# Modulation as row sums on the vector engine, and gate and up products with stationary weights, in a two-block kernel

## The chip, the core and the metric

The kernel runs on one core of a Trainium2 chip, in float32 throughout, in one launch. Five engines run their own instruction streams in order and meet through semaphores: PE (matrix products; PEld is its loading of stationary operands), DVE (vector), ACT (activation functions), POOL, and SP, whose queue here only starts transfers. The metric is the device time of an execution in microseconds (us). The median of three executions of the kernel before is 2738.47 us (2736.33 to 2739.03).

## The reference

256 tokens of width 2048 pass through two blocks; the parts that the change touches:

```python
c_act = jax.nn.silu(c)                                   # c: [1, 2048]
mod = (c_act @ ada_w + ada_b)                            # ada_w: [2048, 6 * 2048]
sh1, sc1, g1, sh2, sc2, g2 = jnp.split(mod, 6, axis=-1)

h = rms_norm(x, norm1_g) * (1 + sc1) + sh1
proj = h @ w_in + b_in                                   # w_in: [2048, 11264]
...                                                      # LRU and attention branches, merged
x = x + g1 * (merged @ w_o)
h2 = rms_norm(x, norm2_g) * (1 + sc2) + sh2
gate, up = jnp.split(h2 @ w_ffn_in, 2, axis=-1)          # w_ffn_in: [2048, 2 * 5632]
x = x + g2 * ((jax.nn.silu(gate) * up) @ w_ffn_out)
x = rms_norm(x, final_g)
...                                                      # second block: gated linear attention
h2 = rms_norm(x, norm_g_2[1])
gate, up = jnp.split(h2 @ ffn_w_gu_2, 2, axis=-1)
x = x + (jax.nn.silu(gate) * up) @ ffn_w_down_2
```

## The kernel before

Activations lie transposed in SBUF: features on the 128 partitions, the 256 tokens along the row, four feature tiles to a buffer `[128, 4, 256]`. `act` holds 24 such slots.

**Products.** Every large weight is read once, in chunks of 512 x 512 (1 MB) that SP starts into `raw` (three buffers). A chunk is split into two float32r parts: ACT copies half a chunk, `[128, 1024]`, to `hi` (L173), and DVE subtracts, `lo = raw - hi` (L175). There are three buffers for each of `hi` and `lo`, so these run up to three halves ahead of PE. A chunk then takes three products, hi x hi, hi x lo and lo x hi, for each of its four 128-row tiles (`accumulate`). In one form the weights are stationary: 128 x 128 of them are loaded, and 256 tokens stream past (L197, L199, L201), 48 matmuls of 256 columns a chunk; the result has features on the partitions. In the other (`tokens=True`) the activations are stationary and 512 weight columns stream past (L190 to L192), 24 matmuls of 512 columns; the result has tokens on the partitions. There are 464 chunks, so 928 splits on DVE. `split` asks the scheduler for high priority (`PREP`), so splits are placed ahead of other work on ACT and DVE.

**Stages.** First the input products of `h` for 10 column groups of `w_in` (40 chunks, accumulators `e` and `part`; the plan goes through the four 512-feature pieces `h[0]` to `h[3]` in turn, so that the first products need `h[0]` alone), with attention after them; then `w_attn_out` (`aops`), the other groups of `w_in` with the LRU (`ups`, `gps`, `glps`), `w_lru_out` (`lops`), `w_o` (`wops`), the first feed-forward layer (`fgps` gate, `fups` up, `fops` down), the second block, and its feed-forward layer.

**Modulation.** `ada_w` has 12 strips of 1024 columns. `matvec` (L234) goes through a strip in 16 steps: each loads 128 rows, `[128, 1024]` (512 KB), into `mvw` (five buffers) and adds them, times the partition's `silu(c)` value, to `mva` on DVE (L245 the first, L247 the others). After the last step PE sums `mva` over the partitions against a column of ones (`reduce`, L259: eight float32 matmuls of one column, which the trace shows as 16 records), and DVE adds the bias into `mod` (L274). Strip 0 runs before anything else. Strips 1 to 3, which each complete the next `h`, run between the input products, their loads started by POOL; strips 4 to 11 are doled out by `pump()` (a credit per chunk) into the stages up to the first feed-forward layer, their loads on SP's queue, among the chunks of `raw`. One more `matvec` makes `fb`, what `shift2` adds to the first gate group, as a row (L255).

**Feed-forward layers.** `swiglu` takes 11 groups of 512 hidden features, six and then five. Gate and up products run in the `tokens` form; ACT takes SiLU of the gate (L718, L963), DVE multiplies by the up product (L724, L969). Since the down product needs features on the partitions, `turned` sends the result back through PE, eight 128 x 128 transposes a group (L666), and ACT and DVE make the hi and lo parts from PSUM (L668, L669). `by_token` (L336) transposes the two norms' factors.

What decides order: instructions are recorded in program order and a scheduler places them on each engine by its own estimate and the priorities; each engine then works through its list in order.

Of the kernel before, what the change touches and what calls it, by code (L numbers as in the profile page):

```python
# [11 lines left out]
F32 = mybir.dt.float32  # L12
# [13 lines left out]
SLOTS, MVS, RAWS, HIS, LOS = 24, 5, 3, 3, 3  # L26
# [9 lines left out]
    ("c", 16), ("norm1_g", 16), ("b_in", 88), ("conv_w", 64), ("conv_b", 16),  # L36
# [13 lines left out]
def block_pair_kernel(ctx: ExitStack, tc: tile.TileContext, a: dict):  # L50
# [47 lines left out]
    x = [xpool.tile([P, 4, T], F32, name=f"x{g}") for g in range(NG)]  # L98
    ident = const.tile([P, P], F32, name="ident")
# [130 lines left out]
    cact = const.tile([P, 16], F32, name="cact")  # L230
    nc.scalar.activation(cact, v("c", 0, 16), AF.Silu)
    mod = const.tile([P, 96], F32, name="mod")

    def matvec(srcs, col, width, done, queue=nc.gpsimd, row=False):  # L234


        state = {}

        def step(k):
            def run():  # L240
                w = mvw.tile([P, width], F32, tag="mvw", name="mvw")
                queue.dma_start(w, srcs[k])
                if k == 0:
                    state["acc"] = slot("mva", shape=[P, width])
# [6 lines left out]
        def reduce():  # L251
            n = width // P
            ps = bank("mvp")
            if row:
                nc.tensor.matmul(ps[:, 0:width], ones, state["acc"], start=True, stop=True)  # L255
                done(ps[:, 0:width])
                return
            for f in range(n):
                nc.tensor.matmul(ps[:, f:f + 1], state["acc"][:, f * P:(f + 1) * P],  # L259
                                 ones[:, 0:1], start=True, stop=True)  # L260
            done(ps[:, 0:n])

        return [step(k) for k in range(NK)] + [reduce]

    def ada_steps(strip, queue=nc.gpsimd):


        def done(ps):
            if strip < 4:
                cols = ((16 + 4 * strip, 0, 4), (4 * strip, 4, 4))  # L270
            else:
                cols = ((8 * strip, 0, 8),)
            for j, p, n in cols:
                nc.vector.tensor_tensor(mod[:, j:j + n], ps[:, p:p + n], v("ada_b", j, n), ALU.add)  # L274

        return matvec([a["ada_w"][strip, k] for k in range(NK)], lambda k: cact[:, k:k + 1],
                      1024, done, queue)
# [34 lines left out]

    def normed(g, gain, inv, shift, name):
        t = slot(name + "t")
        p = Pair(name)
        for f in range(4):
            j = 4 * g + f
            sh = shift[:, j:j + 1]
            nc.vector.scalar_tensor_tensor(t[:, f, :], x[g][:, f, :], gain[:, j:j + 1], inv,
                                           ALU.mult, ALU.mult)  # L320
            nc.scalar.activation(p.hi(f), t[:, f, :], AF.Identity, bias=sh)
            nc.vector.scalar_tensor_tensor(p.lo(f), t[:, f, :], sh, f32(p.hi(f)),
                                           ALU.add, ALU.subtract)
        return p
# [102 lines left out]
    first = ada_steps(0, nc.sync)  # L427
    for st in first[:10]:
        st()
    for g in range(NG):  # L430
        nc.sync.dma_start(x[g], a["xT"][g])
    for st in first[10:]:
        st()
# [5 lines left out]
    h = []  # L439

    def next_h():
        q = len(h)
        sl = slice(4 * q, 4 * q + 4)
        nc.vector.scalar_tensor_tensor(gain1[:, sl], mod[:, 16 + 4 * q:20 + 4 * q], 1.0,
                                       v("norm1_g", 4 * q, 4), ALU.add, ALU.mult)
        h.append(normed(q, gain1, inv1, shift1, "h"))

    next_h()
    nc.sync.dma_start(ident, a["ident"])
    nc.sync.dma_start(amask, a["amask"])  # L450
    bv = slot("bv", shape=[P, 512])
    nc.sync.dma_start(bv, a["bv"])
# [8 lines left out]
    early = {}  # L461
    ga = {}
    attn = []
# [610 lines left out]
```

## Time and profile before

| | |
|---|---|
| median of three executions | 2738.47 us |
| the profiled execution | 2733.5 us, of which its span 2731.7 us |
| instructions in the span | 43911 |
| read from memory | 597.06 MB, 219 GB/s over the span |
| first product of the input stage | 44.86 us |
| last matmul to the end of the span | 4.0 us |

A row of the profile's timeline gives the start and the duration in us, the engine, the line, the operation and its tiles as out<-in. Matmuls overlap, so what one costs is the distance between starts, not its duration. A row of the windows gives a stretch, its length, the busy time of each engine with its count of instructions, the granted clock of PE (1.00 is full), and what the 16 DMA engines did.

### The profile page before, as it was taken

The numbers are of one execution on the slowest core, as the hardware profiler recorded it, in microseconds if no ns is written. First come the engines' busy times: TensorE is split into PE (matmuls) and PEld (weight loads), VectorE is DVE, ScalarE is ACT, GpSimd is POOL, SyncE is SP. The second block draws the span as 40 slices with busy tenths as digits, with TensorE's granted clock in tenths as the row PEclk, the third lists the DMA queues.
The fourth block names the chain that finished last, engine by engine and source line by source line (L and its number), as shares of the span: only waits on it lengthen the run. The fifth ranks groups of instructions, "written<-read, shape, count | busy, mean of one in ns | idle before, by whom it ended". The sixth has DMA issues, their size and how long they took to land.

```text
span 2731.7 us, 43911 instructions
## 1 busy us (share of the span) xinstructions
PE 2680.5 (98%) x18612; PEld 2479.3 (91%) x18612; DVE 1782.3 (65%) x2000; ACT 1310.7 (48%) x1525; POOL 25.7 (1%) x52
## 2 busy tenths in 40 slices
PE   4999999999999999999999999999999999999999
PEld 3999999999999888999888999899988889988899
DVE  8887876888887865444545667866654544444544
ACT  3446637864445444434444545655544444344443
POOL 1100000000000000000000000000000000000000
PEclk9999999999999999999999999999999999999999
DMA  9984696769875866555555544444555555555554
GB/s 351 370 311 147 221 341 226 273 243 351 336 278 194 311 238 217 186 200 187 191 192 185 195 170 170 142 152 171 200 186 187 195 188 188 199 186 194 190 195 161
DMA packets 100166, 602.00 MB, mean 220 GB/s; under 512 B 11121, under 2 KB 11633, under 8 KB 40577
## 3 DMA queue, kind: packets, MB, share of 16 engines
q1 hardware_dynamic: 93056, 574.03, 59.1%
q0 software_dynamic: 6912, 25.17, 2.3%
q8 instruction: 145, 2.38, 0.3%
q14 instruction: 53, 0.43, 0.0%
HBM read 597.06 MB, written 2.10 MB: 219 GB/s over the span
## 4 chain that ended last, share of the span: by engine, by line
PE 95%; DVE 2%; issue 1%; DMA 1%; ACT 1%; SPq 0%; DVEq 0%; ACTq 0%
PE fgps L192 6%; PE fgps L191 6%; PE fgps L190 6%; PE fops L197 6%; PE fups L190 6%; PE fups L192 6%; PE fups L191 6%; PE fops L201 6%; PE fops L199 6%; PE part L197 2%; PE part L199 2%; PE part L201 2%; PE lops L201 1%; PE ups L197 1%; PE wops L197 1%; PE ups L201 1%
## 5 line engine op out<-in xcount | busy, mean ns | idle before, releaser
L175 DVE TENSOR_TENSOR lo<-raw,hi 128x1024 fp32r<-128x1024 f32 x928 | 1134.3, 1224 | 842.9 <-ACT hi L173 841.2
L173 ACT ACTIVATE hi<-raw 128x1024 fp32r<-128x1024 f32 x928 | 983.1, 1060 | 1270.4 <-PE fups L192 274.5
L197 PE MATMUL fops<-hid,hi 128*128 128x256 f32 x1408 | 389.0, 276 | 0.0
L201 PE MATMUL fops<-hid,lo 128*128 128x256 f32 x1408 | 388.7, 276 | 0.0
L199 PE MATMUL fops<-hid,hi 128*128 128x256 f32 x1408 | 388.6, 276 | 0.0
L190 PE MATMUL fups<-hi,h 128*128 128x512 f32 x704 | 274.0, 389 | 0.0
L192 PE MATMUL fups<-hi,h 128*128 128x512 f32 x704 | 273.9, 389 | 0.0
L191 PE MATMUL fups<-lo,h 128*128 128x512 f32 x704 | 273.9, 389 | 0.0
L199 PEld LDWEIGHTS fops<-hid,hi 128*128 128x128 f32 x1408 | 264.3, 188 | 0.1
L197 PEld LDWEIGHTS fops<-hid,hi 128*128 128x128 f32 x1408 | 264.3, 188 | 0.2
L201 PEld LDWEIGHTS fops<-hid,lo 128*128 128x128 f32 x1408 | 264.3, 188 | 0.0
L190 PE MATMUL fgps<-hi,h 128*128 128x512 f32 x672 | 263.5, 392 | 0.0
L192 PE MATMUL fgps<-hi,h 128*128 128x512 f32 x672 | 261.8, 390 | 0.0
L191 PE MATMUL fgps<-lo,h 128*128 128x512 f32 x672 | 261.6, 389 | 0.0
L247 DVE SCALAR_TENSOR_TENSOR mva<-mvw,cact,mva 128x1024 f32<-128x1024 f32 x180 | 230.6, 1281 | 26.6 <-DMA mvw<-ada_w 24.5
L191 PEld LDWEIGHTS fups<-lo,h 128*128 128x128 f32 x704 | 132.2, 188 | 27.4
L190 PEld LDWEIGHTS fups<-hi,h 128*128 128x128 f32 x704 | 132.2, 188 | 27.4
L192 PEld LDWEIGHTS fups<-hi,h 128*128 128x128 f32 x704 | 132.2, 188 | 27.4
L192 PEld LDWEIGHTS fgps<-hi,h 128*128 128x128 f32 x672 | 126.1, 188 | 26.2
L190 PEld LDWEIGHTS fgps<-hi,h 128*128 128x128 f32 x672 | 126.2, 188 | 25.6
L191 PEld LDWEIGHTS fgps<-lo,h 128*128 128x128 f32 x672 | 126.2, 188 | 25.5
L197 PE MATMUL part<-h,hi 128*128 128x256 f32 x512 | 145.2, 284 | 0.0
(322 smaller groups left out, 5410.7 us busy)
## 6 DMA issues: line engine op xcount, KB each, us to landing
raw<-w_in SPq DMA_DIRECT2D x88, 1024.0 KB, 5.7
raw<-w_ffn_in SPq DMA_DIRECT2D x88, 1024.0 KB, 4.9
raw<-ffn_w_gu SPq DMA_DIRECT2D x88, 1024.0 KB, 4.8
mvw<-ada_w SPq DMA_DIRECT2D x144, 512.0 KB, 7.0
raw<-gla_w_in SPq DMA_DIRECT2D x48, 1024.0 KB, 4.9
raw<-w_ffn_out SPq DMA_DIRECT2D x44, 1024.0 KB, 4.8
raw<-ffn_w_down SPq DMA_DIRECT2D x44, 1024.0 KB, 4.9
mvw<-ada_w POOLq DMA_DIRECT2D x48, 512.0 KB, 8.5
```

The costliest lines, as they stand in the source:

```text
L173: nc.scalar.activation(hi, rb, AF.Copy)
L175: nc.vector.tensor_tensor(lo, rb, f32(hi), ALU.subtract)
L190: nc.tensor.matmul(ps[t], xh, hi[:, wk, :], start=fst, stop=False)
L191: nc.tensor.matmul(ps[t], xh, lo[:, wk, :], start=False, stop=False)
L192: nc.tensor.matmul(ps[t], xl, hi[:, wk, :], start=False, stop=lst)
L197: nc.tensor.matmul(o, hi[:, wk, wsl], src.hi(kk), start=fst and f % 2 == 0, stop=False, skip_group_check=True)
L199: nc.tensor.matmul(o, hi[:, wk, wsl], src.lo(kk), start=False, stop=False, skip_group_check=True)
L201: nc.tensor.matmul(o, lo[:, wk, wsl], src.hi(kk), start=False, stop=lst, skip_group_check=True)
L247: nc.vector.scalar_tensor_tensor(state["acc"], w, col(k), state["acc"], ALU.mult, ALU.add)
```

## The change

Two edits, and what follows from them.

**Modulation.** `ada_w` is laid out transposed on the host, so that each of 96 tiles has 128 outputs on the partitions and the 2048 inputs along the row, in two halves of 1024 (512 KB each, so as many loads as before). `silu(c)` is laid out as a row, the same on every partition: `crow`, `[128, 2048]`, a load of 1 MB and an ACT pass at the start. A half is one DVE instruction that multiplies `mvw` by `crow` in place and writes the row's sum to `part` through `accum_out`; a second, one element a partition, adds the two halves and the bias into `mod`. PE and PSUM have no part in it. `h` is made tile by tile (`first_h`): scale tile, shift tile, gain, normed tile, 16 times. `mvw` has four buffers in place of five. The x pieces are loaded first; `ident`, `amask` and `bv` are loaded once the third chunk has been recorded. Until then splits have no raised priority.

**Gate and up.** Both layers' gate and up products use the stationary-weight form, so SiLU and the product with up are already transposed, `split_act` makes hi and lo from SBUF, and `turned` and both `by_token` calls of the norms are gone. `fb` becomes four columns. In the second layer DVE multiplies by the norm's factor from PSUM, ACT takes SiLU, and DVE multiplies once more.

```diff
-SLOTS, MVS, RAWS, HIS, LOS = 24, 5, 3, 3, 3
+SLOTS, MVS, RAWS, HIS, LOS = 24, 4, 3, 3, 3
...
-        at = 48 if tokens else {"hi": 0, "lo": 32}[name]
+        at = 16 if tokens else {"hi": 96, "lo": 0}[name]
...
+    def ada_tile(j, queue):
+
+        part = small.tile([P, 2], F32, tag="adp", name="adp", bufs=4)
+
+        def step(b):
+            def run():
+                w = mvw.tile([P, 1024], F32, tag="mvw", name="mvw")
+                queue.dma_start(w, a["ada_w"][j, b])
+                nc.vector.scalar_tensor_tensor(w, w, 1.0, crow[:, 1024 * b:1024 * (b + 1)],
+                                               ALU.mult, ALU.mult, accum_out=part[:, b:b + 1])
+                if b == 1:
+                    nc.vector.scalar_tensor_tensor(mod[:, j:j + 1], part[:, 0:1], part[:, 1:2],
+                                                   v("ada_b", j), ALU.add, ALU.add)
+            return run
+
+        return [step(0), step(1)]
+
+    def ada_steps(strip):
+        return [st for j in range(8 * strip, 8 * strip + 8) for st in ada_tile(j, nc.sync)]
...
     def gate1(j):
-        sg = slot("sg", shape=[P, 2, 512])
-        ps = project(chunks_of("w_ffn_in", j), gx if j == 0 else h2, "fgps", True)
+        sg = slot("sg")
+        ps = project(chunks_of("w_ffn_in", j), gx if j == 0 else h2, "fgps")
...
     def up1(sg, j):
-        ps = project(chunks_of("w_ffn_in", FG + j), h2, "fups", True)
-        for t in range(2):
-            nc.vector.tensor_tensor(sg[:, t, :], ps[t], sg[:, t, :], ALU.mult)
-        return sg
+        ps = project(chunks_of("w_ffn_in", FG + j), h2, "fups")
+        for b, part in enumerate(halves(sg)):
+            nc.vector.tensor_tensor(part, ps[b], part, ALU.mult)
+        return split_act(sg, "hid")
...
-                gen = turned(up(sg, j))
-                hid.append(next(gen))
-                turns.append(spawn(gen, 2))
+                hid.append(up(sg, j))
...
     def gate2(j):
-        sg = slot("sg", shape=[P, 2, 512])
-        ps = project(chunks_of("ffn_w_gu", j), h2, "fgps", True)
+        sg = slot("sg")
+        ps = project(chunks_of("ffn_w_gu", j), h2, "fgps")
         finish(norm_task)
-        for t in range(2):
-            nc.scalar.activation(sg[:, t, :], ps[t], AF.Silu, scale=norm5["inv"][:, t:t + 1])
-        return sg
+        for b, part in enumerate(halves(sg)):
+            nc.vector.tensor_tensor(part, ps[b], norm5["inv"], ALU.mult)
+        sv = slot("sv")
+        nc.scalar.activation(sv, sg, AF.Silu)
+        for b, part in enumerate(halves(sv)):
+            nc.vector.tensor_tensor(part, part, norm5["inv"], ALU.mult)
+        return sv
```

The slots of `act` move by 128 bytes modulo 512 (a shorter `vec`, a new `crow`); the offsets `at` move by as much, so that `hi`, `lo` and the activations keep their distance to each other modulo 512 bytes.

Where instructions move. On DVE, at the opening: before, the last steps of strip 0 (`mva`), the bias, the norm's reciprocal, the first split, and then the four tiles of `h[0]` (`ht`, `h`).

```order
L247 SCALAR_TENSOR_TENSOR mva<-mvw,cact,mva 128x1024 x5
L274 TENSOR_TENSOR mod<-mvp,vec 128x4 x2
L444 SCALAR_TENSOR_TENSOR gain_102<-mod,vec 128x4
L310 RECIPROCAL inv_189<-inv1s 128x256
L175 TENSOR_TENSOR lo<-raw,hi 128x1024
L319 SCALAR_TENSOR_TENSOR ht<-x_84,gain_102,inv_189 128x256 x3
L322 SCALAR_TENSOR_TENSOR h<-ht,mod,h 128x256 x3
```

The same place on DVE in the changed kernel, where `mvw,adp<-mvw,crow` is a row sum and `mod<-adp` adds two of them:

```order
L241 SCALAR_TENSOR_TENSOR mvw,adp<-mvw,crow 128x1024 x2
L309 RECIPROCAL inv_130<-inv1s 128x256
L244 SCALAR_TENSOR_TENSOR mod<-adp,vec 128x1
L241 SCALAR_TENSOR_TENSOR mvw,adp<-mvw,crow 128x1024 x2
L449 SCALAR_TENSOR_TENSOR gain_101<-mod,vec 128x1
L241 SCALAR_TENSOR_TENSOR mvw,adp<-mvw,crow 128x1024
L244 SCALAR_TENSOR_TENSOR mod<-adp,vec 128x1
L315 SCALAR_TENSOR_TENSOR ht<-x_84,gain_101,inv_130 128x256
L241 SCALAR_TENSOR_TENSOR mvw,adp<-mvw,crow 128x1024
L318 SCALAR_TENSOR_TENSOR h<-ht,mod,h 128x256
```

The first tile of `h` now stands behind 6 row sums, not behind 16 steps and a reduction; the fourth stands behind 18. Up to the 91st split, which belongs to the sixth chunk of `w_attn_out`, the list of DVE holds 69 additions (L247) and 5 first steps (L245) in the profile of before, and 104 row sums and 52 additions to `mod` in the changed kernel: the first four strips are 64 of these, and 40 of the later ones now stand ahead of this point, where before there were about 10.

On PE, in the first feed-forward layer, before: the last products of a gate chunk, the eight transposes of the group before it, and the next chunk.

```order
L190 MATMUL fgps<-hi,h 128x512
L191 MATMUL fgps<-lo,h 128x512
L192 MATMUL fgps<-hi,h 128x512
L666 MATMUL tps<-ident,sg 128x128 x8
L190 MATMUL fgps<-hi,h 128x512
```

In the changed kernel the same engine goes from a group's up products straight to the next gate products, and no transpose stands between any two chunks:

```order
L200 MATMUL fups<-h,hi 128x256
L202 MATMUL fups<-h,lo 128x256
L198 MATMUL fgps<-h,hi 128x256
L200 MATMUL fgps<-h,hi 128x256
L202 MATMUL fgps<-h,lo 128x256
```

All 22 groups lose their eight transposes; each chunk of gate and up has 48 matmuls of 256 columns in place of 24 of 512.

More of the change, by code (lines that the diff above doesn't have):

```diff
@@ L98, in block_pair_kernel @@
     x = [xpool.tile([P, 4, T], F32, name=f"x{g}") for g in range(NG)]
+    crow = xpool.tile([P, D], F32, name="crow")
     ident = const.tile([P, P], F32, name="ident")
@@ L227, in split_act, with matvec @@
         return p
-    cact = const.tile([P, 16], F32, name="cact")
-    nc.scalar.activation(cact, v("c", 0, 16), AF.Silu)
     mod = const.tile([P, 96], F32, name="mod")
-    def matvec(srcs, col, width, done, queue=nc.gpsimd, row=False):
+    def ada_tile(j, queue):
[13 more added lines that the diff above has]
+        return [st for j in range(8 * strip, 8 * strip + 8) for st in ada_tile(j, nc.sync)]
+    def matvec(srcs, col, done):
         state = {}
@@ L251, in reduce @@
         def reduce():
-            n = width // P
             ps = bank("mvp")
[L254 to L258, printed above, removed]
+            for f in range(4):
                 nc.tensor.matmul(ps[:, f:f + 1], state["acc"][:, f * P:(f + 1) * P],
                                  ones[:, 0:1], start=True, stop=True)
-            done(ps[:, 0:n])
+            done(ps[:, 0:4])
         return [step(k) for k in range(NK)] + [reduce]
[L265 to L277, printed above, removed]
     class SumSq:
@@ L311, in inv_rms, with normed_tile @@
         return inv
+    def normed_tile(g, f, p, t, gain, inv, shift):
+        j = 4 * g + f
+        sh = shift[:, j:j + 1]
+        nc.vector.scalar_tensor_tensor(t[:, f, :], x[g][:, f, :], gain[:, j:j + 1], inv,
+                                       ALU.mult, ALU.mult)
+        nc.scalar.activation(p.hi(f), t[:, f, :], AF.Identity, bias=sh)
+        nc.vector.scalar_tensor_tensor(p.lo(f), t[:, f, :], sh, f32(p.hi(f)),
+                                       ALU.add, ALU.subtract)
     def normed(g, gain, inv, shift, name):
@@ L316, in normed @@
         for f in range(4):
[L317 to L323, printed above, removed]
+            normed_tile(g, f, p, t, gain, inv, shift)
         return p
@@ L426, in block_pair_kernel @@
     shift1 = mod[:, 0:16]
-    first = ada_steps(0, nc.sync)
-    for st in first[:10]:
-        st()
     for g in range(NG):
         nc.sync.dma_start(x[g], a["xT"][g])
-    for st in first[10:]:
-        st()
+    nc.sync.dma_start(crow, a["crow"])
+    nc.scalar.activation(crow, crow, AF.Silu)
     ssq = SumSq("ss1")
@@ L439, in block_pair_kernel, with first_h, run @@
     h = []
[L441 to L452, printed above, removed]
+    ht = {}
+    def first_h(q, f, queue):
+        j = 4 * q + f
+        def run():
+            if f == 0:
+                h.append(Pair("h"))
+                ht[q] = slot("ht")
+            nc.vector.scalar_tensor_tensor(gain1[:, j:j + 1], mod[:, 16 + j:17 + j], 1.0,
+                                           v("norm1_g", j), ALU.add, ALU.mult)
+            normed_tile(q, f, h[q], ht[q], gain1, inv1, shift1)
+        return ada_tile(16 + j, queue) + ada_tile(j, queue) + [run]
+    for f in range(4):
+        for st in first_h(0, f, nc.sync):
+            st()
     held, one, two, three = (12, 13), (8, 9, 10), (11, 18, 19), (20, 21)
@@ L482, in block_pair_kernel @@
                     st()
-                if ahead and len(ahead) <= share:
-                    next_h()
                 ahead = ahead[share:]
-                lead[0] = PREP
+                begun += 1
+                if begun == RAWS:
+                    lead[0] = PREP
+                    nc.sync.dma_start(ident, a["ident"])
+                    nc.sync.dma_start(amask, a["amask"])
+                    bv = slot("bv", shape=[P, 512])
+                    nc.sync.dma_start(bv, a["bv"])
                 if q == NG - 1 and k < ks[-1]:
@@ L514, in block_pair_kernel @@
     for strip in (4, 5, 8, 9, 6, 7):
-        steps += ada_steps(strip, nc.sync)
+        steps += ada_steps(strip)
     credit[1] = 1.1
```

93 lines of the change are left out of this document (33 added, 60 removed).

## The prediction

> **What bounds the kernel now.** I read the page's head first, then the windows, then the timeline where the edits lie.
>
> ```profile
> PE 2680.5 (98%) x18612; PEld 2479.3 (91%) x18612; DVE 1782.3 (65%) x2000; ACT 1310.7 (48%) x1525; POOL 25.7 (1%) x52
> ...
> DVE  8887876888887865444545667866654544444544
> ...
> DMA  9984696769875866555555544444555555555554
> ...
> PE 95%; DVE 2%; issue 1%; DMA 1%; ACT 1%; SPq 0%; DVEq 0%; ACTq 0%
> ```
>
> PE is busy throughout and holds 95% of the chain that ended last, so what comes off PE comes off the time, unless another engine stands right behind it. DVE's slices say where it does: 0.8 or so in the first third, 0.4 to 0.5 later. The windows, cut where the 91st split ends (sixth chunk of `w_attn_out`), and DVE's splits, additions and first steps within the first of them:
>
> ```profile
> 0.00:332.20 332.20, 287.75 (x2251) 275.40 (x2252) 276.57 (x406) 165.03 (x242) 25.67 (x52) 0.99 0.74 279
> 332.20:538.70 206.50, 206.50 (x1779) 205.25 (x1778) 162.00 (x173) 126.67 (x172) 0.00 (x0) 1.00 0.75 278
> 538.70:2731.70 2193.00, 2186.26 (x14587) 1998.64 (x14585) 1343.72 (x1423) 1019.04 (x1113) 0.00 (x0) 1.00 0.59 206
> ...
> 0.00:332.20 332.20, 111.02 (x91) 0.99 0.74 279
> ...
> 0.00:332.20 332.20, 87.23 (x69) 0.99 0.74 279
> ...
> 0.00:332.20 332.20, 3.75 (x5) 0.99 0.74 279
> ```
>
> The third number is PE, the fifth DVE. Up to 332.2 us DVE works 276.6 and has 55.6 free; after 538.7 it is 61% busy.
>
> **Part 1: the transposes go.**
>
> ```profile
> 905.93 0.39 PE L192 MATMUL fgps<-hi,h 128*128 128x512 f32 x1
> 906.16 1.03 PE L666 MATMUL tps<-ident,sg 128*128 128x128 f32 x8
> 906.95 0.48 PE L190 MATMUL fgps<-hi,h 128*128 128x512 f32 x1
> 907.27 0.40 PE L191 MATMUL fgps<-lo,h 128*128 128x512 f32 x1
> 907.50 0.39 PE L192 MATMUL fgps<-hi,h 128*128 128x512 f32 x1
> ```
>
> The eight start at 906.16, the next product at 906.95, and that one holds the following back by 0.32 where 0.23 is usual: 0.79 + 0.09 = 0.88 us a group, 22 groups, **19.4 us**. The four transposes of `by_token` are of the same kind and cost under half a microsecond; I leave them out. DVE and ACT do as much for hi and lo as before. The second layer's four more DVE multiplications a group are of 512 elements each, by the splits' pace below some 0.6 us; they fall where DVE is 40% idle, with the next group's eight chunks of PE work as cover. Without that cover they would cost 2.4 us in each of 11 groups.
>
> **Part 2: gate and up in the other form.** The first window holds down products alone (256 columns), the second gate and up alone (512).
>
> ```profile
> 1140.00:1240.00 100.00, 100.00 (x885) 100.00 (x884) 49.32 (x49) 39.22 (x37) 0.00 (x0) 1.00 0.57 198
> 952.00:994.00 42.00, 42.00 (x187) 34.78 (x186) 21.09 (x20) 17.79 (x19) 0.00 (x0) 1.00 0.59 209
> ```
>
> With the overlap of one matmul at the edges that is 100.3 / 885 = 0.1133 us and 42.4 / 187 = 0.2267 us: two of the short for one of the long, to 0.1%. The 4224 long ones become 8448 short ones for **0 us**, within 1 us either way. The second window also shows PEld less busy (34.8 of 42) than the first (100 of 100), where it keeps up all the same.
>
> The Trainium skill (TensorE: Matmul & The Clock Gate, "Wait — 56ns, not 53.3ns?") gives every warm matmul a fixed cost of about 2.5 ns on top of its columns. By it, 4224 matmuls more would add an estimated 10.6 us, and the sum below would be 2731 instead of 2721. The windows disagree: the extra time here grows with the columns.
>
> **Part 3: the reductions leave PE.**
>
> ```profile
> L259 PE MATMUL mvp<-ones,mva 128*128 128x1 f32 x192 | 24.0, 255 | 38.1 <-DVE mva L247 38.1
> ...
> 183.80 1.83 PE mvp L259 x16
> ...
> 394.23 1.68 PE mvp L259 x16
> ...
> 393.96 0.28 PE L201 MATMUL aops<-ya,lo 128*128 128x256 f32 x1
> 394.07 1.84 PE L259 MATMUL mvp<-ones,mva 128*128 128x1 f32 x16
> 395.77 0.36 PE L197 MATMUL ups<-h,hi 128*128 128x256 f32 x1
> 395.98 0.28 PE L199 MATMUL ups<-h,hi 128*128 128x256 f32 x1
> ```
>
> Twelve strips make 192 records. One opens the kernel, three stand in the input stage (the last at 183.8), eight after 332 us. Each of these takes 1.70 to the next product, and that one 0.10 more than 0.113: 1.80 x 8 = **14.4 us**. Those ahead of 332 us are in part 4. For `fb`, two matmuls of 512 columns become four of one column: half a strip's, 0.9 us, for the 1.0 us that two at 0.5 take; nothing.
>
> **Part 4: the front, up to the 91st split.** Here PE's gain would be large: three reductions and the waits for them, and an opening that needs 6 row sums for the first tile in place of 16 steps. But each split must be made by DVE, which goes through its list in order, so I add up DVE's list. Paces come from a stretch in which it never waits:
>
> ```profile
> 98.32 1.22 DVE L175 TENSOR_TENSOR lo<-raw,hi 128x1024 fp32r<-128x1024 f32 x1
> 99.46 2.60 DVE L247 SCALAR_TENSOR_TENSOR mva<-mvw,cact,mva 128x1024 f32<-128x1024 f32 x2
> 101.97 1.22 DVE L175 TENSOR_TENSOR lo<-raw,hi 128x1024 fp32r<-128x1024 f32 x1
> 103.11 1.28 DVE L247 SCALAR_TENSOR_TENSOR mva<-mvw,cact,mva 128x1024 f32<-128x1024 f32 x1
> 104.31 1.22 DVE L175 TENSOR_TENSOR lo<-raw,hi 128x1024 fp32r<-128x1024 f32 x1
> ```
>
> A split takes 1.14 to the next start, an addition 1.20 to 1.25. Of the 276.6 us, 91 splits are 103.7, 69 additions at 1.20 are 82.8, five first steps 3.5; **86.6 us** are other work, which stays. No row shows a row sum. Its nearest:
>
> ```profile
> L593 DVE SCALAR_TENSOR_TENSOR r<-aa,r 128x1024 f32<-128x1024 f32 x4 | 4.9, 1224 | 2.6 <-ACT aa L591 2.6
> ...
> L392 DVE TENSOR_REDUCE st<-s 128x4 f32<-128x1024 f32 x4 | 4.9, 1213 | 0.4 <-ACT s L388 0.4
> ...
> 11.75 0.17 DVE L547 TENSOR_TENSOR lb<-lb,ly 128x16 f32<-128x16 f32 x1
> 11.95 0.17 DVE L548 TENSOR_SCALAR lb<-lb 128x16 f32<-128x16 f32 x1
> ```
>
> With a constant in place of a per-partition scalar the same operation lasts 1224 ns like a split, so 1.14 is the lower end; a reduction over 1024 elements costs no more than that, so summing in passing can be free. Storing the sum is at least a tiny instruction: 0.20 where one waits for the one ahead (11.75 to 11.95), about half where it doesn't. I take 1.14 + 0.10 = 1.24, with 1.14 and 1.44 (a wait before and behind) as ends that count, and 1.14 + 1.21 = 2.35, a second pass, as the far one. The 52 additions to `mod`, each waiting for a sum, take 0.20: 10.4; twelve more `gain` instructions 1.9; nine old bias additions go, 0.9. The list becomes 86.6 + 103.7 + 104 x 1.24 (129.0) + 10.4 + 1.9 - 0.9 = **330.7 us**, plus about 4 us before x and `crow` are there (3.4 MB at some 0.36 MB per us is in by 11 us, ACT's pass over 2048 elements takes two 1.06 us ones, and 9 us of norm and LRU work fill most of that): 334.7.
>
> Transfers press at the same place. The change moves as many bytes of `ada_w` as before, and `crow` on top; on SP's queue the first `raw` load now stands behind six of the sixteen opening loads, not behind all. With four `mvw` buffers instead of five, each transfer has less lead, and on SP's queue a load that waits for its buffer holds the `raw` loads behind it.
>
> ```profile
> DVE mva L247 <- DMA mvw<-ada_w: 24.5, 20, 3.8
> ...
> 0.00:44.00 44.00, 5.49 (x20) 4.59 (x20) 31.32 (x61) 11.92 (x14) 2.97 (x9) 1.00 0.94 359
> 44.00:193.50 149.50, 145.57 (x1150) 142.04 (x1151) 135.11 (x150) 66.10 (x81) 22.69 (x43) 0.98 0.90 350
> ```
>
> Up to the 51st split, at 193.5, the DMA engines moved 44 x 359 + 149.5 x 350 = 68.1 MB at 0.90 to 0.94 of their time. The changed list needs by its own 51st split 71 row sums (37.2 MB), 26 chunks (27.3), x, `crow` and the rest (3.9): 68.4 MB. So transfers alone allow no gain up to there either. Before, DVE waited 20 times for `mvw`, 1.2 us each; for the front I allow 8 us of such waits, between 0 and 15. The 91st split then ends at **342.7, 10.5 us later than before**. PE, with DVE as the bound, has room for all that it saves there.
>
> **The sum.** From 332.2 to the end the kernel before takes 2399.5. Without 14.4 and 19.4 that is 2365.7. Two stretches give some back: up to the 161st split the later row sums nearly fill DVE (about 189 us of work against 200 of PE), and around the 251st to 291st split, where the changed list places 30 row sums and the LRU's work among 40 splits, DVE needs about 113 us against 109 of PE (40 x 24 x 0.1133); 3 us each. So 342.7 + 2371.7 = 2714.4 for a span of 2731.7, **17.3 us less**. The execution profiled took 2733.5, 1.8 beyond its span, and would take 2716. The median of the runs is 5.0 higher, so I predict **2721 us**.
>
> **The rivals.**
>
> *The front is free* (0.12). Row sums at 1.14, additions at 0.10 and no waits: 86.6 + 103.7 + 118.6 + 5.2 + 1 + 4 = 319, 13 us earlier than before. With the savings of parts 1 and 3 and 3 us given back: 44 less, 2695. For it: DVE's rows repeat to a few ns. Against it: the DMA sum.
>
> *The front costs more than PE saves* (0.14, slower). Every 0.1 us on a row sum adds 10.4 us up to the 91st split and about 3 in the later stretches. The forecast's gain is gone at 1.37 us a row sum; at 1.44 with 10 us of waits the front ends at 365.5, 33 us late, and with 12 us given back later the time is 2749. At 2.35 it would be over 2850. For it: DVE is nearly full there, and nothing shows what reading out a sum takes. The Trainium skill (Vector Engine (DVE) Microarchitecture Reference, "Points that are easy to get wrong") says that this operation with two sources that are not bf16 has half the throughput, with no port left for the accumulator; L247 has two such sources and isn't halved, but it has no accumulator. I give that 0.03 of the 0.14.
>
> *The two cancel* (0.14). DMA waits of 20 us in the front, or row sums near 1.33: 2733 to 2744.
>
> *Gate and up don't keep the pace of the down products* (0.05, within the others). If the extra per matmul counted after all, the 10 us of part 2 would be lost: 2731. For it: no `fgps` has yet run in this form. Against it: `fops`, `part`, `ups` all run at 0.113 there.
>
> **How the numbers follow.** The forecast's own case (2704 to 2733) has 0.60. Faster by over 0.2% (below 2733, about what a measurement can tell from no change) holds it and the first rival: 0.72; within 0.2% 0.14; slower 0.14. The range runs from near the free front to the dear one, 2697 to 2749.
>
> **What would show it.** Right: no `tps`, gate and up matmuls 0.113 us apart, row sums of about 1.25 us, DVE with hardly any idle time from 15 us to the 91st split, which ends near 343 and no earlier than 332, and PE's idle time gathered there; from there to the end some 28 us less than 2399.5. Wrong: the 91st split near 320 (a free front), row sums above 1.37, waits of DVE for `mvw` above 15 us, or a gate chunk above 5.5 us.

## The result, and the profile after

The changed kernel takes 2722.5 us (median of 4 runs, 2718.1 to 2725.1) against 2738.8 us for the kernel before beside it: a ratio of 0.9947, 95% interval 0.9935 to 0.9959. The prediction was 2721 us. In a second set of runs (experiment 8) the ratio was 0.9919, 0.9905 to 0.9932. The intervals don't overlap, so the gain differs between sets by more than one set shows; where, is seen below.

The execution profiled took 2725.1 us (span 2723.3), the slowest of its four, so its stretches show less gain than the medians. From the page of the changed kernel: busy time, slices of DVE and DMA, the chain that ended last, and the group of the row sums (times one, busy us, mean ns, idle time ahead and its releaser):

```profile
PE 2652.5 (97%) x22470; PEld 2607.6 (96%) x22470; DVE 1808.8 (66%) x2324; ACT 1312.2 (48%) x1517; POOL 25.7 (1%) x52
...
DVE  7999988965579954544545677867665555455554
...
DMA  8997788855568755555555544345555555555554
...
PE 80%; DVE 8%; DMA 6%; issue 4%; POOL 1%; ACT 0%; SPq 0%; POOLq 0%; DVEq 0%; ACTq 0%
...
L241 DVE SCALAR_TENSOR_TENSOR mvw<-mvw,crow 128x1024 f32<-128x1024 f32 x192 | 232.3, 1220 | 45.2 <-DMA mvw<-ada_w 44.5
```

PE was 95% of the chain before; now 80%, with DVE at 8% and transfers at 6%. The row sum lasts what a split lasts, 1220 ns, and DVE sat 44.5 us waiting for `ada_w`, against 24.5 us before. The same windows as before the change, cut at the 91st and at the 291st split (third number PE, fifth DVE), first for the kernel before, then for the changed one:

```profile
0.00:332.10 332.10, 287.65 (x2250) 275.30 (x2251) 276.47 (x406) 164.93 (x242) 25.67 (x52) 0.99 0.74 279
332.10:903.20 571.10, 570.98 (x4760) 560.15 (x4759) 457.96 (x507) 320.09 (x410) 0.00 (x0) 1.00 0.76 279
903.20:2731.70 1828.50, 1821.88 (x11606) 1643.85 (x11604) 1047.85 (x1090) 825.73 (x874) 0.00 (x0) 1.00 0.55 191
```

```profile
0.00:343.50 343.50, 289.00 (x2198) 270.79 (x2199) 313.20 (x597) 167.64 (x242) 25.67 (x52) 0.98 0.86 321
343.50:921.10 577.60, 567.96 (x4886) 561.28 (x4884) 448.19 (x609) 322.53 (x416) 0.00 (x0) 1.00 0.73 266
921.10:2723.30 1802.20, 1795.49 (x15388) 1775.58 (x15388) 1047.46 (x1121) 822.05 (x860) 0.00 (x0) 1.00 0.54 188
```

The last stretch, with nearly all of gate and up, is 26.3 us shorter. The middle one, which lost six reductions of 1.8 us, is 6.5 us longer, and the first, the front, 11.4 us longer. Part of where the time of these two goes is seen in DVE's waits, first up to the 91st split and then from there to the 161st, at 553.7 (us, times, longest):

```profile
DVE mvw L241 <- DMA mvw<-ada_w: 19.9, 16, 4.0
DVE lo L176 <- ACT hi L174: 3.2, 4, 1.1
...
DVE mvw L241 <- DMA mvw<-ada_w: 20.6, 15, 2.7
DVE lo L176 <- ACT hi L174: 3.1, 2, 1.6
```

The window of that second part:

```profile
343.50:553.70 210.20, 203.65 (x1710) 198.84 (x1708) 184.99 (x274) 124.64 (x168) 0.00 (x0) 1.00 0.87 321
```

185.0 us of work and 20.6 us of waits for `ada_w` fill 205.6 of the 210.2 us. The waits alone are not new. The kernel before had about as many between its 91st and 291st split, here up to the 161st and behind it:

```profile
DVE mva L247 <- DMA mvw<-ada_w: 9.2, 6, 3.8
...
DVE mva L247 <- DMA mvw<-ada_w: 12.6, 10, 2.6
```

Up to its 161st split its DVE had only 162.0 us of work in 206.5, though, and PE was busy for 570.98 of the 571.10 us of the whole stretch. A piece of the changed kernel's DVE timeline from there (start, duration, instruction; in brackets the idle time ahead of it and what ended it):

```profile
346.82 0.21 DVE L244 SCALAR_TENSOR_TENSOR mod<-adp,vec 128x1 f32<-128x1 f32 x1
346.95 1.22 DVE L176 TENSOR_TENSOR lo<-raw,hi 128x1024 fp32r<-128x1024 f32 x1
348.09 1.22 DVE L241 SCALAR_TENSOR_TENSOR mvw<-mvw,crow 128x1024 f32<-128x1024 f32 x1
349.23 0.09 DVE L241 DVE_READ_ACCUMULATOR mvw<-mvw,crow 128x1 f32 x1
349.23 1.22 DVE L176 TENSOR_TENSOR lo<-raw,hi 128x1024 fp32r<-128x1024 f32 x1
353.10 1.23 DVE L241 SCALAR_TENSOR_TENSOR mvw<-mvw,crow 128x1024 f32<-128x1024 f32 x1 [2.65 <-DMA mvw<-ada_w]
354.25 0.08 DVE L241 DVE_READ_ACCUMULATOR mvw<-mvw,crow 128x1 f32 x1
354.25 1.22 DVE L176 TENSOR_TENSOR lo<-raw,hi 128x1024 fp32r<-128x1024 f32 x1
```

Behind the row sum at 348.09 the next split starts at 349.23: the read of the accumulator runs beside it, and a row sum takes 1.14 in all. An addition to `mod` takes 0.13 (346.82 to 346.95). At 350.45 DVE stops 2.65 us for a tile of `ada_w`; the next split stands behind it in the queue and can't pass. Here PE still had finished splits and lost only 0.2 us, at 355.5; a stop that cost it 2 us is shown under experiment 9.

All kernels of the study, by profile, in us; ratios are medians against the kernel before in the same set of runs:

| kernel | row sums ahead of 91st split | 51st split | 91st split | 91st to 291st | 291st to end | ratio |
|---|---|---|---|---|---|---|
| before | none (73 steps) | 193.5 | 332.1 | 571.1 | 1828.5 | 1 |
| changed | 104 | 199.7 | 343.5 | 577.6 | 1802.2 | 0.9947 |
| changed, second set | 104 | 195.1 | 338.8 | 572.8 | 1802.1 | 0.9919 |
| 1 gate and up alone | none (73 steps) | 191.5 | 330.2 | 575.7 | 1808.4 | 0.9925 |
| 2 modulation alone | 104 | 194.2 | 339.5 | 574.2 | 1824.3 | 1.0014 |
| 3 old front, new later | 37 (+ 64 steps) | 208.5 | 354.1 | 575.7 | 1802.2 | 0.9983 |
| 4 first strip row sums | 53 (+ 48 steps) | 202.7 | 348.6 | 577.3 | 1802.2 | 0.9980 |
| 5 paced | 72 | 191.3 | 329.3 | 571.9 | 1804.7 | 0.9883 |
| 6 mixed, paced | 24 (+ 48 steps) | 210.7 | 348.6 | 566.3 | 1804.7 | 0.9944 |
| 7 five buffers | 107 | 191.0 | 335.5 | 577.9 | 1803.0 | 0.9926 |
| 9 paced by tile | 69 | 192.7 | 330.7 | 575.4 | 1804.7 | 0.9906 |
| 10 the same, five buffers | 69 | 190.0 | 327.9 | 566.4 | 1805.0 | 0.9868 |
| 11 later sums left out | 64 | 192.1 | 329.9 | 559.9 | 1804.7 | 0.9854 |
| 12 mixed, paced, five buffers | 24 (+ 48 steps) | 196.6 | 334.6 | 568.1 | 1805.1 | 0.9903 |

### The profile page after: what moved, and what is told of

Its sections match the earlier page's. It is cut to its first block, busy times and chain, and to the rows that moved or that the text cites. A ratio compares the mean times of both kernels' runs of the same rounds, so it can differ in the third digit from the quotient of the medians.

```text
span 2723.3 us, 51982 instructions
## 1 busy us (share of the span) xinstructions
PE 2652.5 (97%) x22470; PEld 2607.6 (96%) x22470; DVE 1808.8 (66%) x2324; ACT 1312.2 (48%) x1517; POOL 25.7 (1%) x52
## 4 chain that ended last, share of the span: by engine, by line
PE 80%; DVE 8%; DMA 6%; issue 4%; POOL 1%; ACT 0%; SPq 0%; POOLq 0%; DVEq 0%; ACTq 0%
PE fops L198 6%; PE fops L202 6%; PE fops L200 6%; PE fups L200 6%; PE fups L202 6%; PE fups L198 6%; PE fgps L202 5%; PE fgps L200 5%; PE fgps L198 5%; DMA mvw<-ada_w 5%; DVE lo L176 3%; DVE mvw L241 2%; PE ggps L200 1%; PE glps L200 1%; PE grps L198 1%
## 5 line engine op out<-in xcount | busy, mean ns | idle before, releaser
L202 PE MATMUL fups<-h,lo 128*128 128x256 f32 x1408 | 388.9, 276 | 0.1
L200 PE MATMUL fups<-h,hi 128*128 128x256 f32 x1408 | 388.8, 276 | 0.2 <-DVE h L318 0.2
L198 PE MATMUL fups<-h,hi 128*128 128x256 f32 x1408 | 388.6, 276 | 0.0
L202 PE MATMUL fgps<-h,lo 128*128 128x256 f32 x1344 | 371.4, 276 | 0.8 <-DVE lo L176 0.5
L198 PE MATMUL fgps<-h,hi 128*128 128x256 f32 x1344 | 371.2, 276 | 0.0
L200 PE MATMUL fgps<-h,hi 128*128 128x256 f32 x1344 | 371.0, 276 | 0.0
L202 PEld LDWEIGHTS fups<-h,lo 128*128 128x128 f32 x1408 | 264.3, 188 | 0.5 <-DVE lo L176 0.5
L200 PEld LDWEIGHTS fups<-h,hi 128*128 128x128 f32 x1408 | 264.3, 188 | 0.4 <-DVE h L318 0.4
L198 PEld LDWEIGHTS fups<-h,hi 128*128 128x128 f32 x1408 | 264.3, 188 | 0.0
L241 DVE SCALAR_TENSOR_TENSOR mvw<-mvw,crow 128x1024 f32<-128x1024 f32 x192 | 232.3, 1220 | 45.2 <-DMA mvw<-ada_w 44.5
L202 PEld LDWEIGHTS fgps<-h,lo 128*128 128x128 f32 x1344 | 252.3, 188 | 1.4 <-DVE lo L176 1.4
L200 PEld LDWEIGHTS fgps<-h,hi 128*128 128x128 f32 x1344 | 252.3, 188 | 0.0
L198 PEld LDWEIGHTS fgps<-h,hi 128*128 128x128 f32 x1344 | 252.3, 188 | 0.0
L202 PE MATMUL part<-h,lo 128*128 128x256 f32 x512 | 143.1, 279 | 4.4 <-DVE lo L176 4.4
```

Source lines behind the costliest of these rows:

```text
L198: nc.tensor.matmul(o, hi[:, wk, wsl], src.hi(kk), start=fst and f % 2 == 0, stop=False, skip_group_check=True)
L200: nc.tensor.matmul(o, hi[:, wk, wsl], src.lo(kk), start=False, stop=False, skip_group_check=True)
L202: nc.tensor.matmul(o, lo[:, wk, wsl], src.hi(kk), start=False, stop=lst, skip_group_check=True)
L241: nc.vector.scalar_tensor_tensor(w, w, 1.0, crow[:, 1024 * b:1024 * (b + 1)], ALU.mult, ALU.mult, accum_out=part[:, b:b + 1])
```

## The experiments

**1 and 2: the two edits apart.** Gate and up alone, on the kernel before:

```diff
-        ps = project(chunks_of("w_ffn_in", j), gx if j == 0 else h2, "fgps", True)
+        ps = project(chunks_of("w_ffn_in", j), gx if j == 0 else h2, "fgps")
...
-                gen = turned(up(sg, j))
+                hid.append(up(sg, j))
```

> The kernel before with the edit of the gate and up products alone; the modulation stays as it was, and fb is kept as columns. Theory A (the products keep the pace and the transposes were all cost; the rest of the change is what gave back): 19.4 us less than the kernel before, about 2719 us, the 91st split within 2 us of 332. Theory B (the shorter matmuls or the added DVE work took part of it, 10 us by a fixed cost per matmul): 9 us less, about 2730 us, and matmuls of fgps over 0.114 us apart.

Measured: 2714.8 against 2735.4 us, 0.9925 (0.9911 to 0.9939), 20.7 us less; the 91st split at 330.2. Theory A. Its profile has the stretch from the 91st to the 291st split 4.6 us longer than the kernel before, though no row sum stands in it.

The modulation alone, on the changed kernel:

```diff
-        ps = project(chunks_of("w_ffn_in", j), gx if j == 0 else h2, "fgps")
+        ps = project(chunks_of("w_ffn_in", j), gx if j == 0 else h2, "fgps", True)
...
-                hid.append(up(sg, j))
+                gen = turned(up(sg, j))
```

> The changed kernel with the gate and up products as they were before (512 columns, transposes); the modulation as row sums alone. Theory A: the two edits add up, so 16.2 us of gain less 19.4 leaves a loss of 3 us, about 2742 us, with the 91st split near 343. Theory B: 7 us less than before, about 2731 us.

Measured: 2739.7 us, 1.0014 (1.0002 to 1.0026), 4.3 us more; the 91st split at 339.5. The edits add up: 20.7 less and 4.3 more make 16.4 us, and the change gained 16.2 (20.3 in the second set, 4 us from the sum). The row sums as a whole lose a little, their interval just clear of no change: their eight reductions saved on PE are more than paid back.

**3 and 4: row sums only where they looked free.** Two mixtures on the changed kernel, with four buffers; `strip_steps` is the old accumulation with its reduction on PE. In the second, strip 0 keeps its row sums.

```diff
-            ahead = [st for f in range(4) for st in first_h(q + 1, f, nc.gpsimd)]
+            ahead = strip_steps(q + 1) + [next_h]
...
+    nc.sync.dma_start(crow, a["crow"])
+    nc.scalar.activation(crow, crow, AF.Silu)
     for strip in (4, 5, 8, 9, 6, 7):
         steps += ada_steps(strip)
```

> Gate and up as in the change; the first four strips of the modulation as accumulated products with the reduction on PE, as before (with four buffers instead of five); the eight later strips as row sums, with crow loaded after the input stage. Theory A (the front of the change lost 10 to 11 us, and the later strips gain up to 14.4 us on PE and give part of it back where DVE is full): the 91st split at 332 to 335, then 2706 us if nothing is given back, 2712 with the 6 us that the prediction gave back, 2719 if all that the changed kernel lost after its 91st split comes from the row sums themselves. Theory C (what was lost after the 91st split was only a consequence of the late front): 2706 us, and DVE's splits between the 91st and the 291st never further behind the kernel before than at the 91st.

> As the kernel with the old front, but the strip that opens the kernel is made by row sums as in the change; strips two to four by accumulated products with the reduction on PE. If DVE's list is what bounds the front, the first product starts some 15 us earlier, the 16 row sums and 8 additions cost DVE about 4 us, and the 91st split ends 8 to 12 us earlier than 332, for 2698 to 2708 us. If transfers bound the front, the 91st split ends at 330 to 335 all the same and the time is that of the kernel with the old front.

Measured: 2731.4 us, 0.9983 (0.9974 to 0.9992), and 2730.2 us, 0.9980 (0.9971 to 0.9989). None of the theories foresaw the 91st split at 354.1 and 348.6. DVE's list up to there, counted in the first mixture's trace, had 37 row sums of the later strips in it, where the old form had 9 steps of strip 4. That gave a new theory, D: an old step waits for the accumulator of the step ahead, and a strip for a slot and for its reduction; row sums wait for nothing but their tile, so the scheduler draws those of later strips forward into stretches where DVE or the transfers are already full. The changed kernel has 40 of them ahead of the 91st split, and all 96 of strips 4 to 9 ahead of the 161st, where the kernel before has the last step of these strips behind the 237th. Part of the delay in both mixtures has another cause: the 51st split is already 9 to 15 us late (experiment 12).

**5 and 6: the later row sums kept at their place.** The 1.0 of each group of four tiles is made from the block just finished:

```diff
+    def release(n):
+        nc.vector.tensor_scalar(gain1[:, n:n + 1], recent[0], 0.0, 1.0, ALU.mult, ALU.add)
...
-                nc.vector.scalar_tensor_tensor(w, w, 1.0, crow[:, 1024 * b:1024 * (b + 1)],
+                nc.vector.scalar_tensor_tensor(w, w, one, crow[:, 1024 * b:1024 * (b + 1)],
...
         z.append(ga[f])
+        recent[0] = ga[f][:, 0, 0:1]
```

> The changed kernel, with the row sums of strips 4 to 11 kept at their place in the program: each group of four tiles multiplies by a 1.0 that is made from the result of the block just finished, in place of the constant 1.0. In DVE's order 72 row sums then stand ahead of the 91st split instead of 104, and 104 ahead of the 161st instead of 160. Theory D (the later strips' row sums, which no accumulator holds back any more, were drawn forward into stretches where DVE is the bound): 32 fewer at about 1.3 us each take 42 us off DVE's list up to the 91st split, which ends at 305 to 325 instead of 343, and nothing more is given back up to the 291st; the time is 2685 to 2705 us. Theory E (transfers, or the 64 row sums of the input stage themselves, set the front): the 91st split stays at 335 or later, and the time at 2716 us or more.

> As the kernel whose first strip is made by row sums and strips two to four by accumulated products, with the later strips' row sums kept at their place in the same way: 72 modulation steps ahead of the 91st split instead of 101. Theory D: the 91st split at 305 to 325 instead of the 350 or so that it has without the pacing, time 2688 to 2708 us, within 6 us of the paced row sums throughout (DVE saves about 0.1 us on each of 48 steps, PE pays three reductions of 1.8 us). Theory E: 340 or later, and 2722 us or more.

Measured for the paced changed kernel: 2704.4 against 2734.7 us, 0.9883 (0.9869 to 0.9897), below the changed kernel beside it (0.9905 to 0.9932). The time lies at the edge of what theory D gave, its steps do not: the 91st split came to 329.3 instead of 305 to 325, 9.5 us earlier than beside it, and 571.9 us to the 291st still hold 11.6 that were given back (571.1 less 10.8 would be 560.3). The windows up to and behind the 51st split, of the changed kernel's second set and then of the paced one, show why:

```profile
0.00:195.10 195.10, 148.95 (x1126) 140.44 (x1127) 176.08 (x327) 80.47 (x96) 25.66 (x52) 1.00 0.96 362
195.10:338.80 143.70, 136.82 (x1054) 127.30 (x1054) 136.73 (x272) 86.30 (x145) 0.00 (x0) 0.99 0.75 275
```

```profile
0.00:191.30 191.30, 146.94 (x1105) 138.44 (x1106) 168.45 (x310) 79.44 (x95) 25.67 (x52) 1.00 0.94 359
191.30:329.30 138.00, 136.19 (x1074) 127.98 (x1073) 109.28 (x208) 86.48 (x146) 0.00 (x0) 1.00 0.54 188
```

Behind the 51st split DVE is full in the changed kernel (136.7 of 143.7) and is not when paced (109.3 of 138.0); but PE has 136 us of work there in either, so 27 us less on DVE are worth 5.7. Up to the 51st split the DMA engines are busy 0.94 to 0.96 of the time, and there the two differ by 3.8. Behind the 91st split pacing gained nothing: from there to the end the paced kernel takes 2376.6 us, the changed one beside it 2374.9. The waits for `ada_w` only moved: up to the 161st split they fell from 17.1 to 3.2 us, from there to the 291st they rose from 0.5 to 22.4.

The mixture missed: 2721.1 us, 0.9944 (0.9930 to 0.9957), and its 51st split came later with the pacing, at 210.7 instead of 202.7. From the 51st to the 91st split pacing gained as much here as above, 8.0 us (145.9 to 137.9).

**7 and 8: a fifth buffer, and the changed kernel again.**

```diff
-SLOTS, MVS, RAWS, HIS, LOS = 24, 4, 3, 3, 3
+SLOTS, MVS, RAWS, HIS, LOS = 23, 5, 3, 3, 3
```

> The changed kernel with five buffers for the tiles of ada_w instead of four (and 23 slots instead of 24). If the lead of the transfers is what made DVE wait 43 us for ada_w, the waits fall below 25 us, the 91st split ends 5 to 10 us earlier than 343 and the time is about 2714 us. By theory D the same row sums are drawn forward (105 ahead of the 91st split), and the time stays within 5 us of the changed kernel's.

> The changed kernel itself beside these three, on the same chip: about 0.994 of the kernel before, the 91st split within 4 us of 343.

Measured: 2715.2 us, 0.9926 (0.9914 to 0.9939), against 2714.4 us, 0.9919 (0.9905 to 0.9932). Both theories gave about this time, so it doesn't decide between them. With five buffers the front is 3.3 us shorter and the stretch to the 291st split 5.1 us longer. DVE's waits for `ada_w` in the front, with four buffers and with five, and between the 91st and the 161st split with four and with five:

```profile
DVE mvw L241 <- DMA mvw<-ada_w: 16.7, 12, 4.2
...
DVE mvw L241 <- DMA mvw<-ada_w: 17.1, 13, 2.6
```

```profile
DVE mvw L241 <- DMA mvw<-ada_w: 9.3, 6, 3.7
...
DVE mvw L241 <- DMA mvw<-ada_w: 16.8, 11, 4.2
```

The buffer shortens the waits in the front and not those behind it: with 107 row sums drawn forward DVE stays full, with 182.4 us of work and 16.8 of these waits in the 210.8 us between the two splits. Up to the 291st split the waits are 32.6 us in all, not below 25 as the first theory had them.

**9 and 10: released tile by tile, with four and with five buffers.**

```diff
-            n = (j - 32) // 4
-            out += ada_tile(j, nc.sync, gain1[:, n:n + 1], n if j % 4 == 0 else None)
+            n = j - 32
+            out += ada_tile(j, nc.sync, gain1[:, n % 16:n % 16 + 1], n)
```

> The kernel with paced row sums, released tile by tile (two row sums each) instead of four tiles at once. In the kernel with groups of four, PE lost 10.8 us in gps, glps, lops and wops beyond 0.1134 us a matmul between the 91st and the 291st split. Theory D1 (eight row sums let go at once keep a split waiting, which has only 3 lo buffers as cover): these fall to under 4 us, and the time is about 7 us less than with groups of four: a ratio to the kernel before of 0.986. Rival (they come from DVE's fill in the stretch as a whole): no change, 0.988 to 0.989.

> The same with five buffers for ada_w and 23 slots. If the floor of the front is transfers (68.4 MB by the 51st split at 350 MB per ms, 191 us), the 51st split stays at 188 to 192 and the time within 3 us of the kernel with four buffers; if the fewer buffers in flight set it, the 51st split ends at 183 or earlier, and the time is 5 to 10 us less.

Measured with four buffers: 2709.8 us, 0.9906 (0.9891 to 0.9920); theory D1 fell, what PE lost in `gps`, `glps`, `lops` and `wops` beyond 0.1134 us between matmul starts rose to 16.7 us, from 11.7 in the same count for groups of four. One of the losses, in DVE's timeline and then in PE's:

```profile
743.34 1.28 DVE L248 SCALAR_TENSOR_TENSOR mvw<-mvw,gain,crow 128x1024 f32<-128x1024 f32 x1
744.55 0.08 DVE L248 DVE_READ_ACCUMULATOR mvw<-mvw,gain,crow 128x1 f32 x1
744.66 0.22 DVE L251 SCALAR_TENSOR_TENSOR mod<-adp,vec 128x1 f32<-128x1 f32 x1
744.80 1.22 DVE L176 TENSOR_TENSOR lo<-raw,hi 128x1024 fp32r<-128x1024 f32 x1
749.87 1.28 DVE L248 SCALAR_TENSOR_TENSOR mvw<-mvw,gain,crow 128x1024 f32<-128x1024 f32 x1 [3.85 <-DMA mvw<-ada_w]
751.08 0.08 DVE L248 DVE_READ_ACCUMULATOR mvw<-mvw,gain,crow 128x1 f32 x1
751.08 1.22 DVE L176 TENSOR_TENSOR lo<-raw,hi 128x1024 fp32r<-128x1024 f32 x1
...
750.25 0.28 PE L200 MATMUL lops<-yr,hi 128*128 128x256 f32 x1
752.36 0.39 PE L202 MATMUL lops<-yr,lo 128*128 128x256 f32 x1 [1.82 <-DVE lo L176]
```

Here it is not the row sums ahead of a split that hold it, but one row sum's missing tile: DVE stops 3.85 us at 746.02, the split behind it starts at 751.08, and at 750.3 PE stands still for 2 us in `lops`. These waits between the 91st and 291st split, with four buffers and with five:

```profile
DVE mvw L248 <- DMA mvw<-ada_w: 19.5, 11, 3.9
...
DVE mvw L248 <- DMA mvw<-ada_w: 9.4, 4, 2.7
```

With five the time is 2699.5 us, 0.9868 (0.9853 to 0.9883): the fastest complete kernel of the study, its interval below both of the changed kernel's, though it overlaps that of the paced one with groups of four. The 51st split came at 190.0, where it was expected if transfers set it, and that although the first split ended at 48.9, 21 us later than with four buffers. The time is 10.3 us less, where at most 3 was expected; 9.0 of that lies between the 91st and the 291st split.

**11: the row sums of strips 4 to 11 left out.**

```diff
                 queue.dma_start(w, a["ada_w"][j, b])
+                if out:
+                    if b == 1:
+                        nc.vector.tensor_copy(mod[:, j:j + 1], v("ada_b", j))
+                    return
```

> The changed kernel without the row sums of strips 4 to 11: their tiles of ada_w are still loaded, but mod takes ada_b alone there. Theory D (the later row sums on DVE cost the front 10 us and gave back what the reductions saved after it): the 91st split ends at 325 to 330 instead of 339 to 343, and from there to the end some 2366 us instead of the changed kernel's 2375 and 2380 (2399.6 less 19.4 and 13.6); the time about 2694, a ratio of 0.984 to 0.986. If the loss after the 91st split has another cause (the loads on SP's queue, the gate and up products), 2374 or more from there, and 0.988 or more.

Measured: 2695.9 us, 0.9854 (0.9840 to 0.9869). Its windows:

```profile
0.00:329.95 329.95, 282.98 (x2178) 266.10 (x2179) 271.66 (x561) 165.99 (x241) 25.78 (x52) 1.00 0.95 358
329.95:889.80 559.85, 559.85 (x4878) 558.08 (x4878) 356.37 (x409) 322.35 (x415) 0.00 (x0) 1.00 0.71 264
889.80:2694.50 1804.70, 1798.07 (x15418) 1778.46 (x15417) 1038.36 (x1099) 824.10 (x861) 0.00 (x0) 1.00 0.53 187
```

All tiles are still loaded, even faster than in the changed kernel (358 GB/s up to the 91st split, against 321). PE is never idle between the 91st and the 291st split, and 559.9 is 11.2 us less than before the change: six reductions at 1.8 are 10.8. From the 91st split to the end it takes 2364.6, where theory D gave 2366. So the loads do no harm by themselves; the row sums do. By which route isn't separated here: without them DVE loses 92 us of work in the middle stretch (448.2 to 356.4) and all its waits for `ada_w`, and SP no longer waits for a row sum to free a buffer (22.2 us there in the changed kernel, none here).

**12: the mixture of experiment 6 with five buffers and 23 slots.**

> The kernel with strip one by row sums, strips two to four by accumulated products, and the later row sums paced by four tiles, with five buffers instead of four (23 slots). With four its 51st split ended at 210.7, against 193.5 of the kernel before with five buffers and the same kind of steps. If the accumulated steps on POOL's queue need the fifth buffer, the 51st split comes to 190 to 196, the 91st to 328 to 334 and the ratio to about 0.987; if the later start of strip two's steps or the reductions on PE made it late, 205 or later and 0.993 to 0.995.

Measured: 2709.9 us, 0.9903 (0.9887 to 0.9920), the 51st split at 196.6 and the 91st at 334.6. The 51st and 91st splits lie within 1 us of what was expected if the fifth buffer was needed; the ratio was to be 0.987. The edit accounts for 14.1 us of the 17.2 that this mixture was late at the 51st split. It also reorders the opening, where the first split ends at 51.9 instead of 29.4. The granted clock of PE up to the 51st split was 0.89 with four buffers and 0.99 with five, but that is hardly the reason: over their spans the other four executions with four buffers were granted 0.997, the profiled one 0.992, and they took 2718.8 to 2722.6 us against its 2721.4. Of the 17.2, 3 us are left, for which the reductions on PE are one candidate. It also means that experiments 3 and 4 tested two things at once: of the first mixture's 22 us at the 91st split, 15.0 were there at the 51st, ahead of which it has a single row sum, and 7.0 came behind it, with the other 36.

## Why the prediction was right

**Transposes and the pace of gate and up (19.4 and 0 us): right.** Experiment 1 gained 20.7 us, and in its profile the stretch behind the 291st split is 20.1 shorter. A window of the changed kernel with gate and up alone:

```profile
1000.00:1042.00 42.00, 42.00 (x373) 42.00 (x372) 20.99 (x20) 18.62 (x20) 0.00 (x0) 1.00 0.54 192
```

With the overlap at the edges that is 42.3 / 373 = 0.1134 us a matmul, half of the 0.2267 of the long ones. The Trainium skill (TensorE: Matmul & The Clock Gate, "Wait — 56ns, not 53.3ns?") has a fixed 2.5 ns on each warm matmul, which would have cost an estimated 10.6 us here; the trace shows none of it. The added work of DVE and ACT stayed hidden behind PE, as said.

**Reductions (14.4 us): right, where nothing pays them back.** Experiment 11 shows 11.2 for six, experiment 2 shows 4.2 for the two behind the 291st split.

**The front (342.7): right number, from two errors that cancel and half a reason.** The 91st split came at 343.5 and, in the second set, 338.8. A row sum was priced at 1.24; its pace is 1.14, the low end given. The additions to `mod` were priced at 0.20; they take 0.13. These two make the list 104 x 0.10 + 52 x 0.07 = 14 us shorter than the 330.7 worked out; DVE's busy time was 313.2, another 3.5 less. Against these 17.5, idle time was 30.3 us instead of 4 + 8, so 18.3 more, of it 19.9 for `ada_w`: more than the 15 that the prediction named as a sign against it. That the two come out even is luck. The 8 us allowed for load waits had no row of the front behind it: of the 24.5 us that the prediction cites, 1.6 lay ahead of the 91st split. The rivals that turn on the price of a row sum are out: the gain was to be gone at 1.37. The half throughput of the Trainium skill (Vector Engine (DVE) Microarchitecture Reference, "Points that are easy to get wrong") doesn't show: 1220 ns, with two float32 sources and an accumulator read.

The reason given, that DVE's list bounds the whole front, holds only from the 51st split on, where 27 us of it were worth 5.7 us. Up to the 51st split all kernels with four buffers and the change's own order of loads in the input stage, and those with five, end at 190 to 200 us, near the 193.5 of before, whether the first split ends at 28 or at 52 us; the kernel before had 27 us of idle DVE there. The second half of the argument, 68.4 MB of transfers, fits these runs: rate times time gives 68 to 71 MB at 352 to 373 GB/s (paced, 191.3 us at 359 GB/s are 68.7 MB; at 350, 68.4 MB would take 195 us, not the 191 in the expectation of experiment 10). DVE, with 166 to 177 us of work, was nearly full there too, and a kernel with cheaper row sums in the input stage wasn't tried, so the two aren't separated by an experiment.

**The later stretches (6 us given back): too small; this step failed.** "Up to the 161st split the later row sums nearly fill DVE (about 189 us of work against 200 of PE)": the work was right, 185.0, but the 20.6 us of waits for `ada_w` on top were left out; load waits were allowed for in the front only. Without row sums this stretch to the 291st split takes 559.9; the changed kernel took 577.6 and 572.8, so 17.7 and 12.9 us were given back (17.3 and 12.5 against 571.1 less 10.8). Against experiment 11, the place up to the 161st split cost 8.5 and 8.0 us in the two sets (210.2 and 209.7 against 201.7), where 3 was forecast; the place from the 251st to the 291st split cost 7.7 and 3.2 (117.3 and 112.8 against 109.6), where 3 was forecast.

Ahead of the 91st split there is a cause that the prediction counted without naming it: it put 104 row sums there, 31 more steps than before, and took them as given. Kept at their place, they give back 9.5 us up to that split, and with five buffers they leave a kernel 0.5 to 0.8% faster than the changed one.

For the middle stretch the cause stays open in part. Experiment 11 shows that the row sums cost the time there, and the pair 9 and 10 that a fifth buffer, with 10.1 us fewer waits, takes 9.0 us off it. But the total of the waits doesn't set the loss. Against 560.3 the mixtures of experiments 6 and 12 lost 6.0 and 7.8 us with 21.2 and 17.3 us of waits, the paced kernel 11.6 with 25.6, the changed one 17.3 with 23.5, and in the kernel before, with 21.8, PE was hardly idle. Experiment 1, with no row sums, was also 4.6 us longer there, so some of it differs between executions.

**The sum.** The execution profiled was to take 2716 and took 2725.1: 11.3 us more were given back than forecast, 0.9 more was lost in the front, and 3.3 more were gained behind the 291st split (26.3 for 23.0; the paced kernels gain 23.8 there, so the splits of the unpaced ones probably stand closer to PE at that point, which wasn't tested). The median came out at 2722.5 for 2721 since the 5.0 us that the prediction added, as in the kernel before, turned out as 2.6 less; that it lies within 1.5 us is luck, since the second set's median is 2714.4. In the second set the span is 2713.7 for the 2714.4 forecast, with 6.7 us lost in the front for 10.5, and 12.5 given back for 6. (The dear end of the range adds up to 2750, not 2749: 365.5 + 2365.7 + 12 + 1.8 + 5.0.)

## What to carry to other kernels

A chain of dependent steps also paces: when a change makes steps independent, count how many of them the new order puts ahead of the work that sets the time, not only what each costs. An instruction that may wait for a load should not stand ahead of critical work in an in-order queue without enough buffers in flight. Its busy time says nothing of that price; the waits have to be added, and then compared with the room that the engine has left: 21.8 us of waits cost nothing before the change, where DVE had room. A front that starts 15 us earlier (the first split ends at 28.4 instead of 43.9) was worth nothing 150 us later here, where the transfers came to the same 68 to 71 MB either way.

## What the runs showed of the hardware

Reading out the sum cost nothing in pace: the record of 83 ns lies beside the next instruction, which starts 1.14 us after the row sum did, as after a split. The Trainium skill (VectorE: DVE Perf Modes, "Two Vector instructions with no wait between them") counts an operation that also writes out its accumulator as two instructions; the trace has both records. With the scalar read from memory instead of a constant the same row sum takes 1.21 (743.34 to 744.55), 0.06 to 0.07 more: some 8 or 9 us over the 128 paced ones.

The two sets of the changed kernel differ by 9.6 us in span, all of it ahead of the 291st split (4.7 up to the 91st, 4.8 from there), and their waits of DVE for `ada_w` by 9.1 us (43.4 against 34.3); behind it they agree to 0.1 us. In these two profiles the stretch that PE alone bounds repeats, and those in which transfers and DVE press don't.
